# Down stage of a fused block kernel: W11 loaded once into the tile that becomes T1, T2 and T4, ten places in turn for the other blocks, T4's sums begun in P3

## The chip, the cores and the metric

One Trainium2 chip, one core. The metric is the device time of one execution in microseconds (us); lower is better.

## What is computed

The reference is one transformer block on x (512 x 2048, fp32): AdaLN modulation, a convolution mixer and a sparse attention mixer, an output projection, and a gated feed-forward network. The change touches only the last matrix product, the one with ffn_w2:

```python
h = modulate(rms_norm(x, norm_ffn[l]), sh_f, sc_f)
x = x + g_f[:, None, :] * ((silu(h @ ffn_w1[l]) * (h @ ffn_w3[l])) @ ffn_w2[l])   # ffn_w2: 5632 x 2048
```

## The kernel before

The stage for the last product, here the down stage, multiplies the gated activations (512 x 5632, spilled to DRAM as `gd` by the stage before it, here the up stage) by `ffn_w2`. It splits both into 2 x 2 blocks and forms seven products P1 to P7 in place of eight (Strassen's scheme in Winograd's form). The 5632 rows of `ffn_w2` are cut into four groups b = 0 to 3 (`GS = (5, 6, 6, 5)`). In each group a block of the weight has 5 or 6 tiles of 128 x 1024 (512 KB), indexed j. The order of the products is 1, 2, 5, 6, 3, 7, 4 in group 0 and 1, 5, 6, 3, 7, 2, 4 in the others. One tile of one product is a unit (b, p, j): 12 matmuls of 512 columns on PE. There are 154 units, written out in `units`; the loop at the end of the listing walks over them.

What a product needs of the weight: P1 takes W11, P2 takes W21, P3 takes W22, P5 takes T1, P6 takes T2 and P4 takes T4. T1 is W11 + W12 (the plain load of W11 on SP's queue, then an accumulating DMA of W12 on POOL's queue), T2 is T1 + W22 (a DVE addition, `w_sum`), T4 is T2 + W21 (an accumulating DMA on POOL's queue). All three are the same tile `t` in turn. P7 takes T3 = W12 + W22, a load on SP's queue and an accumulating DMA on POOL's queue into a tile of its own. (`"t3"` in the code; the sums' signs lie in the other operand.)

Every unit's weight tile is then split by `w_split`: ACT casts it to the matmul's type (`whi`, `w_hi`, L948), DVE subtracts (`wlo`, L1262). `hi` and `lo` have three buffers each, so the split of unit n + 2 can begin when PE has done with unit n - 1. The activations are split in the same way by `a_parts` (`ghi` on ACT, `glo` on DVE), and `evict` adds the PSUM banks to the output tiles on DVE after each product.

Where the tiles lie: W11 in `ring[0]` (tag raw, 4 places, shared with the up stage), t in `tz` (6 places), and W22, T3 and W21 in `wz` (tag w, 6 places). `tz`, `wz` and the activations' parts lie in memory that the up stage's operands hC1 to hC7 have held. `AHEAD` says how many units ahead of its own a tile's load is written in the program (W11 4, T1 9, W22 6, T3 7, W21 6, T4's sum 10); within that, a scheduler orders each engine's queue, and a load waits until the last reader of its place is done. SP's and POOL's queues issue in order: an issue that waits holds back what stands behind it. `r`, `gd` and `gf` on SP's queue are the up stage's spill, the residual and the gate; `k` on POOL's queue is the load of the next group's activations.

Of the kernel before, what the change touches and what calls it, by code (L numbers as in the profile page):

```python
# [9 lines left out]
F32 = mybir.dt.float32  # L10
# [3 lines left out]
ALU = mybir.AluOpType  # L14
# [3 lines left out]
P = 128  # L18
# [51 lines left out]
def block_kernel(ctx: ExitStack, tc: tile.TileContext, a: dict, out: bass.AP):  # L70
    nc = tc.nc
# [4 lines left out]
    def pool(name, bufs=1, stack=ctx, **kw):  # L76
        return stack.enter_context(tc.tile_pool(name=name, bufs=bufs, reuse_waits="tile", **kw))
# [4 lines left out]
    def rings(stack, raw, split):  # L82
        return (pool("raw", raw, stack=stack), pool("hi", split, stack=stack), pool("lo", split, stack=stack))
# [42 lines left out]
    ring = rings(ctx, 4, 3)  # L126
# [752 lines left out]
    for n in range(4):  # L879
# [8 lines left out]
        for i, ps in enumerate(pst):  # L888
            t = tp.tile([P, 512], F32, tag="t", name="t")
# [56 lines left out]
    def w_hi(t):  # L946
        hi = ring[1].tile([P, HK * P], F32R, tag="hi", name="whi")
        nc.scalar.copy(hi, t)  # L948
        return hi
# [156 lines left out]
    GS, GM, HN = (5, 6, 6, 5), 6, D // 2  # L1106
# [4 lines left out]
    def k_load(b, half):  # L1111
        n = GS[b]
        t = kraw[b, half] = krp.tile([P, GM, S], F32, tag=f"k{half}", name=f"k{half}")
        for j in range(n):
            nc.gpsimd.dma_start(t[:, j, :], gd[START[b] + half * n + j])
# [73 lines left out]
    tz = pool("tz", GM)  # L1189
    wz = pool("wz", 6)  # L1190
# [4 lines left out]
    W, A_, bank = {}, {}, {}  # L1195

    def a_parts(b, p):

        with tc.issue_after(W["last"]) if W.get("last") else ExitStack():
            a_parts_(b, p)  # L1200
# [26 lines left out]
    def w_load(b, p, j):  # L1227
        f = (START[b] + j, START[b] + GS[b] + j)

        def block(r, c):  # L1230
            return w2[f[r] * P:(f[r] + 1) * P, c * HN:(c + 1) * HN]

        def get(pl, tag, one, plus=None):
            t = pl.tile([P, HN], F32, tag=tag, name=tag)
            nc.sync.dma_start(t, one)
            if plus is not None:
                nc.gpsimd.dma_start(t, plus, accum_op=ALU.add)
            return t

        if p == 1:  # L1240
            W[b, 11, j] = get(ring[0], "raw", block(0, 0))
        elif p == 5:
            W[b, "t", j] = get(tz, "t", block(0, 0), block(0, 1))
        elif p == 6:
            W[b, 22, j] = get(wz, "w", block(1, 1))
        elif p == 7:
            W[b, "t3", j] = get(wz, "w", block(0, 1), block(1, 1))
        elif p == 2:
            W[b, 21, j] = get(wz, "w", block(1, 0))
        elif p == 4:  # L1250
            nc.gpsimd.dma_start(W[b, "t", j], block(1, 0), accum_op=ALU.add)

    def w_sum(b, p, j):
        if p == 6:
            t = W[b, "t", j]
            nc.vector.tensor_add(t, t, W[b, 22, j])

    def w_split(b, p, j):
        t = W[b, {1: 11, 5: "t", 6: "t", 3: 22, 7: "t3", 2: 21, 4: "t"}[p], j]
        hi = w_hi(t)  # L1260
        lo = ring[2].tile([P, HN], F32R, tag="lo", name="wlo")
        W["last"] = nc.vector.tensor_sub(lo, t, hi.bitcast(F32)).ins  # L1262
        W[b, p, j] = hi, lo
# [5 lines left out]
    def multiply(b, p, js, done=None):  # L1269
        name, make = banks(b, p)  # L1270
        if 0 in js and p in (1, 5, 2):
            bank[name] = [make() for _ in range(4)]
        ps = bank[name]
        ahi, alo = A_[b, p]
        for t in range(2):
            tok = slice(t * P, (t + 1) * P)
            for c in range(2):
                cs = slice(c * 512, (c + 1) * 512)
                for j in js:
                    hi, lo = W[b, p, j]  # L1280
                    for m, (x_, w) in enumerate(((ahi, lo), (alo, hi), (ahi, hi))):
                        nc.tensor.matmul(ps[2 * t + c], x_[:, j, tok], w[:, cs],  # L1282
                                         start=m == 0 and j == 0 and p in (1, 5, 2),
                                         stop=m == 2 and j == GS[b] - 1 and p in (3, 2, 4), skip_group_check=True)
                if done:
                    done(t, c)

    def evict(b, p):
        last = b == NG - 1
        r, c = {1: (0, 0), 2: (0, 0), 6: (0, 1), 3: (0, 1), 5: (1, 1), 7: (1, 1), 4: (1, 0)}[p]  # L1290
        if b == 0 and p == 1:
            return
        for t in range(2):
            for h in range(2):
                cs = slice(c * HN + h * 512, c * HN + (h + 1) * 512)
                y = y2[2 * r + t][:, cs]
                ps = bank[banks(b, p)[0]][2 * t + h]
                if b == 0 and p in (2, 5, 6, 4):
                    nc.scalar.copy(y, ps)
                else:  # L1300
                    nc.vector.tensor_add(y, ps, y)
                if last and p in (3, 7, 2):
                    nc.vector.scalar_tensor_tensor(y, y, -1.0 if c else 1.0, gf[:, cs], op0=ALU.mult, op1=ALU.mult)
            if last and p in (3, 7, 2):
                i = 2 * r + t
                nc.gpsimd.dma_start(out[0, i * P:(i + 1) * P, c * HN:(c + 1) * HN], y2[i][:, c * HN:(c + 1) * HN],
                                    accum_op=ALU.add)
        if b == 0 and p == 2:

            for t in range(2):  # L1310
                for h in range(2):
                    y = y2[t][:, h * 512:(h + 1) * 512]
                    nc.vector.tensor_add(y, bank["x"][2 * t + h], y)

    def last_block():

        for t in range(2):
            for h in range(2):
                cs = slice(h * 512, (h + 1) * 512)
                y = y2[2 + t][:, cs]  # L1320
                r = dp.tile([P, 512], F32, tag=f"d{1 + h}", name="r")
                nc.sync.dma_start(r, xd[h][:, t, :])
                nc.vector.tensor_mul(y, y, gf[:, cs])
                nc.vector.tensor_add(y, y, r)
# [8 lines left out]

    prods = [(b, p) for b in range(NG) for p in ((1, 5, 6, 3, 7, 2, 4) if b else (1, 2, 5, 6, 3, 7, 4))]
    units = [(b, p, j) for b, p in prods for j in range(GS[b])]
    AHEAD = {1: 4, 5: 9, 6: 6, 7: 7, 2: 6, 4: 10}

    def loads(n):
        for m in range(n + 13, n + 3, -1):
            if 0 <= m < len(units):  # L1340
                b, p, j = units[m]
                if (12 if (b, p) == (0, 5) else AHEAD.get(p)) == m - n:
                    w_load(b, p, j)

    for n in range(-13, 0):
        loads(n)
    for m in range(2):
        w_split(*units[m])
    a_parts(*prods[0])
    with tc.issue_after(A_["last"]), tc.issue_after(A_["first"]):  # L1350
        order[-1]["post"](order[-1])
# [2 lines left out]
    for n, (b, p, j) in enumerate(units):  # L1354
        last = b == NG - 1
        if j == 0:
            q += 1
            if q + 2 < len(prods):
                a_parts(*prods[q + 2])
        if j == 2:  # L1360
            if not last and p == 3:
                k_load(b + 1, 0)
            elif not last and q % 7 == 5:
                k_load(b + 1, 1)
            elif last and p == 6:
                gf = krp.tile([P, GM, S], F32, tag="k0", name="k0").rearrange("p j s -> p (j s)")[:, :D]
                nc.sync.dma_start(gf, gfd.to_broadcast([P, D]))
        loads(n)
        if n + 4 < len(units):
            w_sum(*units[n + 4])  # L1370
        if n + 2 < len(units):
            w_split(*units[n + 2])
        if last and p == 4:
            if j == 0:
                last_block()
            if j < GS[b] - 3:
                multiply(b, p, [j])
            elif j == GS[b] - 1:
                multiply(b, p, [j - 2, j - 1, j], last_tile)
            continue  # L1380
        multiply(b, p, [j])
        if j == GS[b] - 1:
            evict(b, p)
# [24 lines left out]
```

## Time and profile before

| | |
|---|---|
| median of 3 runs | 2261.0 us (2258.97 to 2263.16) |
| the profiled execution's own time | 2263.49 us |
| its span, first to last instruction | 2261.7 us |
| PE busy | 96% of the span |
| mean granted clock of TensorE | 0.991 of full speed |
| first and last matmul of the down stage | 1792.42 and 2256.8 us |

The span is what the trace covers; the execution's own time is 1.8 us longer. PE's busy time is modelled from the starts of its matmuls. An engine's idle time matters here only where PE waits for it in the end.

### The profile page before, as it was taken

How to read it: one execution, taken by the hardware profiler on the slowest of the kernel's cores; microseconds unless marked ns; L12 is line 12 of the kernel's file. 1: busy time of each engine (PE TensorE's matmuls, PEld its weight loads, DVE VectorE, ACT ScalarE, POOL GpSimd, SP SyncE). 2: the span in 40 equal slices, each digit the busy share in tenths (PEclk: the TensorE clock that was granted, in tenths of full speed). 3: DMA queues.
4: the chain of work that ended last, by engine and by line, in shares of the span. 5: the costliest groups of instructions: out<-in, count | busy, mean ns of one | idle time of the engine just before them, and what ended most of it. 6: DMA issues, size and time to landing. Idle time of an engine off the chain costs nothing.

```text
span 2261.7 us, 30554 instructions
## 1 busy us (share of the span) xinstructions
PE 2182.5 (96%) x11377; PEld 1812.0 (80%) x11377; DVE 1725.9 (76%) x2523; ACT 996.1 (44%) x1558; POOL 222.4 (10%) x267
## 2 busy tenths in 40 slices
PE   6999999999999999899999999999999998999998
PEld 5788778778777787788888888888888876777786
DVE  6878877877769755977878777887878776778697
ACT  5335235554444222744444444444444454444442
POOL 5310000000000000010000000000000121211111
PEclk9999999999999999999999999999999999999999
DMA  9965766544446865397776767677775699786966
GB/s 319 363 219 178 260 198 189 165 143 137 135 138 223 296 233 160 104 224 174 180 183 165 184 170 179 165 177 172 182 182 135 208 292 264 180 265 176 265 155 161
DMA packets 441096, 446.72 MB, mean 198 GB/s; under 512 B 18232, under 2 KB 345116, under 8 KB 440308
## 3 DMA queue, kind: packets, MB, share of 16 engines
q1 hardware_dynamic: 371764, 330.40, 46.7%
q0 software_dynamic: 69040, 114.12, 23.6%
q8 instruction: 89, 1.46, 0.3%
q14 instruction: 59, 0.48, 0.1%
q10 hardware_dynamic: 144, 0.26, 0.0%
HBM read 424.78 MB, written 19.93 MB: 197 GB/s over the span
## 4 chain that ended last, share of the span: by engine, by line
PE 73%; DMA 12%; DVE 11%; issue 2%; ACT 1%; POOL 0%; SPq 0%; DVEq 0%; ACTq 0%; POOLq 0%
PE main L960 14%; PE aux L960 10%; PE main L962 7%; PE main L98 6%; PE main L100 6%; PE main L99 6%; PE aux L1282 5%; PE aux L962 5%; DMA araw<-in_ada_w 5%; PE main L1282 5%; DMA w<-in_ffn_w 5%; DVE acc L185 2%; DVE wlo L1262 2%; PE aux L98 1%; DMA raw<-in_ffn_w 1%
## 5 line engine op out<-in xcount | busy, mean ns | idle before, releaser
L948 ACT CAST whi<-raw 128x1024 fp32r<-128x1024 f32 x282 | 295.3, 1047 | 351.5 <-PE main L960 114.0
L953 DVE TENSOR_TENSOR wlo<-raw,whi 128x1024 fp32r<-128x1024 f32 x260 | 315.4, 1218 | 81.2 <-ACT whi L948 80.8
L960 PE MATMUL main<-hC,whi 128*128 128x512 f32 x1408 | 356.7, 395 | 5.2 <-DVE hC L977 3.7
L960 PEld LDWEIGHTS main<-hC,whi 128*128 128x128 f32 x1408 | 255.1, 190 | 51.9 <-DVE hC L977 4.3
L960 PE MATMUL aux<-hC,whi 128*128 128x512 f32 x1072 | 270.1, 393 | 0.0
L185 DVE SCALAR_TENSOR_TENSOR acc<-araw,cT,acc 128x512 f32<-128x512 f32 x248 | 185.6, 748 | 73.2 <-DMA araw<-in_ada_w 60.2
L960 PEld LDWEIGHTS aux<-hC,whi 128*128 128x128 f32 x1072 | 193.7, 190 | 34.9
L962 PEld LDWEIGHTS main<-hC,wlo 128*128 128x128 f32 x1408 | 192.1, 190 | 13.8
L962 PE MATMUL main<-hC,wlo 128*128 128x256 f32 x1408 | 196.3, 282 | 0.0
L98 PE MATMUL main<-alo,whi 128*128 128x512 f32 x448 | 182.8, 408 | 1.4 <-DVE alo L347 1.4
L948 ACT CAST whi<-t 128x1024 fp32r<-128x1024 f32 x108 | 113.5, 1052 | 152.7 <-PE aux L1282 42.1
L99 PE MATMUL main<-ahi,wlo 128*128 128x512 f32 x448 | 176.6, 394 | 0.0
L100 PE MATMUL main<-ahi,whi 128*128 128x512 f32 x448 | 176.5, 395 | 0.0
L92 ACT CAST whi<-raw 128x1024 fp32r<-128x1024 f32 (+2 forms) x84 | 79.5, 949 | 207.0 <-PE main L100 138.6
L962 PEld LDWEIGHTS aux<-hC,wlo 128*128 128x128 f32 x1072 | 146.3, 190 | 12.4 <-DVE wlo L953 1.9
L98 PE MATMUL main<-wlo,ahi 128*128 128x512 f32 x384 | 152.9, 398 | 0.0
L99 PE MATMUL main<-whi,alo 128*128 128x512 f32 x384 | 151.8, 395 | 0.0
L962 PE MATMUL aux<-hC,wlo 128*128 128x256 f32 x1072 | 149.9, 282 | 1.5 <-DVE wlo L953 1.5
L100 PE MATMUL main<-whi,ahi 128*128 128x512 f32 x384 | 151.1, 394 | 0.0
L1262 DVE TENSOR_TENSOR wlo<-w,whi 128x1024 fp32r<-128x1024 f32 x66 | 79.9, 1222 | 81.3 <-ACT whi L948 81.2
L1282 PE MATMUL aux<-wlo,ghi 128*128 128x512 f32 x308 | 123.1, 400 | 16.2 <-DVE wlo L1262 16.2
L1049 DVE TENSOR_TENSOR raw<-raw 128x1024 f32<-128x1024 f32 x84 | 102.3, 1218 | 47.1 <-DMA raw<-in_ffn_w 47.0
(317 smaller groups left out, 4069.5 us busy)
## 6 DMA issues: line engine op xcount, KB each, us to landing
raw<-in_ffn_w SPq DMA_DIRECT2D x219, 512.0 KB, 4.9
araw<-in_ada_w SPq DMA_DIRECT2D x176, 256.0 KB, 3.0
w<-in_ffn_w SPq DMA_DIRECT2D x66, 512.0 KB, 8.0
t<-in_ffn_w POOLq DMA_DIRECT2D x65, 512.0 KB, 8.5
araw<-in_ada_w POOLq DMA_DIRECT2D x56, 512.0 KB, 14.4
raw<-in_w_in SPq DMA_DIRECT2D x128, 192.0 KB, 2.7
t<-in_ffn_w SPq DMA_DIRECT2D x43, 512.0 KB, 5.7
araw<-in_ada_w SPq DMA_DIRECT2D x40, 512.0 KB, 5.4
```

Source lines behind the costliest of these rows:

```text
L92: nc.scalar.copy(hi[:, :m], raw[:, :m])
L98: nc.tensor.matmul(ps, lhs[0], rhs[1], start=first, stop=False)
L99: nc.tensor.matmul(ps, lhs[1], rhs[0], start=False, stop=False)
L100: nc.tensor.matmul(ps, lhs[0], rhs[0], start=False, stop=last)
L185: nc.vector.scalar_tensor_tensor(acc, w, s, acc, op0=ALU.mult, op1=ALU.add)
L948: nc.scalar.copy(hi, t)
L953: nc.vector.tensor_sub(lo, t, hi.bitcast(F32))
L960: nc.tensor.matmul(ps, wt[0][:, ks[k]], hC[p][:, k, :], start=first and k == 0, stop=False, skip_group_check=True)
L962: nc.tensor.matmul(ps[:, HS:], wt[1][:, ks[k]], hC[p][:, k, 0:HS], start=False, stop=last and k == HK - 1, skip_group_check=True)
L1049: nc.vector.tensor_add(to, x, y)
L1262: W["last"] = nc.vector.tensor_sub(lo, t, hi.bitcast(F32)).ins
L1282: nc.tensor.matmul(ps[2 * t + c], x_[:, j, tok], w[:, cs], start=m == 0 and j == 0 and p in (1, 5, 2), stop=m == 2 and j == GS[b] - 1 and ...
```

## The change

W11 is loaded by `w_load` for P1 straight into the tile t, P1 splits it there, and right behind the split of each P1 unit POOL is given the accumulating DMA that makes T1 of it (`split`). The separate load of W11 for T1 is gone: 22 loads of 512 KB fewer. W22, T3 and W21 take ten places in turn, four in `ring[0]` and six in `wz` (`place`). The leads are longer: W11 5, W22 9, T3 12, W21 9 (7 in group 0), T4's sum 15 (14 in group 0), so that it is written beside P3.

```diff
--- before.py
+++ after.py
@@ -1230,23 +1230,26 @@
         def block(r, c):
             return w2[f[r] * P:(f[r] + 1) * P, c * HN:(c + 1) * HN]
 
-        def get(pl, tag, one, plus=None):
-            t = pl.tile([P, HN], F32, tag=tag, name=tag)
+        def place():
+            W["n"] = W.get("n", -1) + 1
+            pl, tag = (ring[0], "raw") if W["n"] % 10 < 4 else (wz, "w")
+            return pl.tile([P, HN], F32, tag=tag, name=tag)
+
+        def get(t, one):
             nc.sync.dma_start(t, one)
-            if plus is not None:
-                nc.gpsimd.dma_start(t, plus, accum_op=ALU.add)
             return t
 
         if p == 1:
-            W[b, 11, j] = get(ring[0], "raw", block(0, 0))
+            W[b, "t", j] = get(tz.tile([P, HN], F32, tag="t", name="t"), block(0, 0))
         elif p == 5:
-            W[b, "t", j] = get(tz, "t", block(0, 0), block(0, 1))
+            nc.gpsimd.dma_start(W[b, "t", j], block(0, 1), accum_op=ALU.add)
         elif p == 6:
-            W[b, 22, j] = get(wz, "w", block(1, 1))
+            W[b, 22, j] = get(place(), block(1, 1))
         elif p == 7:
-            W[b, "t3", j] = get(wz, "w", block(0, 1), block(1, 1))
+            t = W[b, "t3", j] = get(place(), block(0, 1))
+            nc.gpsimd.dma_start(t, block(1, 1), accum_op=ALU.add)
         elif p == 2:
-            W[b, 21, j] = get(wz, "w", block(1, 0))
+            W[b, 21, j] = get(place(), block(1, 0))
         elif p == 4:
             nc.gpsimd.dma_start(W[b, "t", j], block(1, 0), accum_op=ALU.add)
 
@@ -1256,7 +1259,7 @@
             nc.vector.tensor_add(t, t, W[b, 22, j])
 
     def w_split(b, p, j):
-        t = W[b, {1: 11, 5: "t", 6: "t", 3: 22, 7: "t3", 2: 21, 4: "t"}[p], j]
+        t = W[b, {1: "t", 5: "t", 6: "t", 3: 22, 7: "t3", 2: 21, 4: "t"}[p], j]
         hi = w_hi(t)
         lo = ring[2].tile([P, HN], F32R, tag="lo", name="wlo")
         W["last"] = nc.vector.tensor_sub(lo, t, hi.bitcast(F32)).ins
@@ -1333,19 +1336,24 @@
 
     prods = [(b, p) for b in range(NG) for p in ((1, 5, 6, 3, 7, 2, 4) if b else (1, 2, 5, 6, 3, 7, 4))]
     units = [(b, p, j) for b, p in prods for j in range(GS[b])]
-    AHEAD = {1: 4, 5: 9, 6: 6, 7: 7, 2: 6, 4: 10}
+    AHEAD = {1: 5, 6: 9, 7: 12, 2: 9, 4: 15}
 
     def loads(n):
-        for m in range(n + 13, n + 3, -1):
+        for m in range(n + 16, n + 3, -1):
             if 0 <= m < len(units):
                 b, p, j = units[m]
-                if (12 if (b, p) == (0, 5) else AHEAD.get(p)) == m - n:
+                if (7 if (b, p) == (0, 2) else 14 if b == 0 and p == 4 else AHEAD.get(p)) == m - n:
                     w_load(b, p, j)
 
-    for n in range(-13, 0):
+    def split(n):
+        w_split(*units[n])
+        if units[n][1] == 1:
+            w_load(units[n][0], 5, units[n][2])
+
+    for n in range(-16, 0):
         loads(n)
     for m in range(2):
-        w_split(*units[m])
+        split(m)
     a_parts(*prods[0])
     with tc.issue_after(A_["last"]), tc.issue_after(A_["first"]):
         order[-1]["post"](order[-1])
@@ -1369,7 +1377,7 @@
         if n + 4 < len(units):
             w_sum(*units[n + 4])
         if n + 2 < len(units):
-            w_split(*units[n + 2])
+            split(n + 2)
         if last and p == 4:
             if j == 0:
                 last_block()
```

SP's queue where the up stage ends, before: raw_16056 and raw_16058 (ahead of these rows), raw_16063, raw_16070 and raw_16104 are W11 of group 0; raw_16728 is W11 of group 1, t_16060 and t_16065 the first tiles of T1, w_16068 the first of W21.

```order
L1235 DMA raw_16063<-in_ffn_w2 128x1024
L1012 DMA gd42_6762<-d2_15719 128x512
L1322 DMA r_19113<-xd0_6718 128x512
L1322 DMA r_19117<-xd1_6719 128x512
L1235 DMA raw_16070<-in_ffn_w2 128x1024
L1235 DMA raw_16104<-in_ffn_w2 128x1024
L1235 DMA raw_16728<-in_ffn_w2 128x1024
L1235 DMA t_16060<-in_ffn_w2 128x1024
L1235 DMA t_16065<-in_ffn_w2 128x1024
L1235 DMA w_16068<-in_ffn_w2 128x1024
```

The same place now: raw_16099 and raw_16122 are the third and fourth tile of W21, the five t are W11 of group 0, w_16141 is the last tile of W21, w_16217 the first of W22.

```order
L1239 DMA raw_16099<-in_ffn_w2 128x1024
L1012 DMA gd42_6762<-d2_15719 128x512
L1325 DMA r_19069<-xd0_6718 128x512
L1325 DMA r_19073<-xd1_6719 128x512
L1239 DMA raw_16122<-in_ffn_w2 128x1024
L1239 DMA t_16056<-in_ffn_w2 128x1024
L1239 DMA t_16058<-in_ffn_w2 128x1024
L1239 DMA t_16060<-in_ffn_w2 128x1024
L1239 DMA t_16064<-in_ffn_w2 128x1024
L1239 DMA t_16068<-in_ffn_w2 128x1024
L1239 DMA w_16141<-in_ffn_w2 128x1024
L1239 DMA w_16217<-in_ffn_w2 128x1024
```

W21 has moved ahead of W11, and the first tile of W11, which stood first, now stands behind the fourth of the `raw` loads.

DVE's queue at the same time, before: wlo_16074, wlo_16078 and wlo_16108 are P1's units 0 to 2, glo_16081 is P1's activations, glo_16090 P2's and glo_16096 P5's; d1 and d2 belong to the up stage's last tile.

```order
L1262 TENSOR_TENSOR wlo_16078<-raw_16058,whi_16076 128x1024
L967 TENSOR_TENSOR d1_15861<-aux_15997,d1_15861 128x256
L1213 TENSOR_TENSOR e_16093<-k1_15928,k0_15922 128x1280
L1262 TENSOR_TENSOR wlo_16108<-raw_16063,whi_16106 128x1024
L1224 TENSOR_TENSOR glo_16081<-k0_15922,ghi_16080 128x1280
L971 TENSOR_TENSOR d1_15861<-main_15844,d1_15861 128x256
L1224 TENSOR_TENSOR glo_16090<-k1_15928,ghi_16089 128x1280
L1079 SCALAR_TENSOR_TENSOR d2_15885<-d2_15885,d1_15861 128x512
L1224 TENSOR_TENSOR glo_16096<-e_16093,ghi_16095 128x1280
```

And now, where wlo_16072, wlo_16077 and wlo_16103 are P1's units 0 to 2:

```order
L967 TENSOR_TENSOR d1_15861<-aux_15997,d1_15861 128x256 x2
L1265 TENSOR_TENSOR wlo_16072<-t_16056,whi_16070 128x1024
L1265 TENSOR_TENSOR wlo_16077<-t_16058,whi_16075 128x1024
L1224 TENSOR_TENSOR glo_16081<-k0_15922,ghi_16080 128x1280
L971 TENSOR_TENSOR d1_15861<-main_15844,d1_15861 128x256
L1224 TENSOR_TENSOR glo_16090<-k1_15928,ghi_16089 128x1280
L1079 SCALAR_TENSOR_TENSOR d2_15885<-d2_15885,d1_15861 128x512
L1213 TENSOR_TENSOR e_16093<-k1_15928,k0_15922 128x1280
L1265 TENSOR_TENSOR wlo_16103<-t_16060,whi_16101 128x1024
```

P1's activations now follow two splits of W11 tiles that the changed SP queue has loaded late. Behind these rows DVE's order is the same in both kernels to the end.

SP's queue ahead of group 1, before: t_16843 and t_16864 are the last tiles of T1 of group 1, raw_16821 and raw_16846 of its W11; the four raw_17... are W11 of group 2, and w_17147, w_17174 the first tiles of T3 of group 1.

```order
L1235 DMA t_16843<-in_ffn_w2 128x1024
L1235 DMA t_16864<-in_ffn_w2 128x1024
L1235 DMA raw_16821<-in_ffn_w2 128x1024
L1235 DMA raw_16846<-in_ffn_w2 128x1024
L1235 DMA raw_17571<-in_ffn_w2 128x1024
L1235 DMA raw_17592<-in_ffn_w2 128x1024
L1235 DMA raw_17613<-in_ffn_w2 128x1024
L1235 DMA raw_17634<-in_ffn_w2 128x1024
L1235 DMA w_17147<-in_ffn_w2 128x1024
L1235 DMA w_17174<-in_ffn_w2 128x1024
```

And now: raw_17043 to w_17102 are the first four tiles of T3 of group 1, the five t its W11 tiles 1 to 5, w_17121 and w_17140 the last two of T3.

```order
L1239 DMA raw_17043<-in_ffn_w2 128x1024
L1239 DMA raw_17063<-in_ffn_w2 128x1024
L1239 DMA raw_17083<-in_ffn_w2 128x1024
L1239 DMA w_17102<-in_ffn_w2 128x1024
L1239 DMA t_16720<-in_ffn_w2 128x1024
L1239 DMA t_16738<-in_ffn_w2 128x1024
L1239 DMA t_16756<-in_ffn_w2 128x1024
L1239 DMA t_16775<-in_ffn_w2 128x1024
L1239 DMA t_16803<-in_ffn_w2 128x1024
L1239 DMA w_17121<-in_ffn_w2 128x1024
L1239 DMA w_17140<-in_ffn_w2 128x1024
```

Four of the six T3 loads have moved from behind the next group's first W11 loads to ahead of their own group's W11.

## Rows read from the trace of the kernel before

**Rows 1.** The page: PE's line of part 1 (busy us, share of the span, instructions) and part 4, the chain that ended last, by engine.

```profile
PE 2182.5 (96%) x11377; PEld 1812.0 (80%) x11377; DVE 1725.9 (76%) x2523; ACT 996.1 (44%) x1558; POOL 222.4 (10%) x267
...
PE 73%; DMA 12%; DVE 11%; issue 2%; ACT 1%; POOL 0%; SPq 0%; DVEq 0%; ACTq 0%; POOLq 0%
```

**Rows 2.** Who waited for whom from 1790 to 2262 us: us in total, times, longest.

```profile
ACT whi L948 <- DMA w<-in_ffn_w: 80.8, 25, 7.4
...
PE aux L1282 <- DVE wlo L1262: 16.2, 12, 3.7
PE main L1282 <- DVE wlo L1262: 14.7, 12, 4.7
```

**Rows 3.** PE's matmuls of the down stage (L1282) in stretches that begin and end at the first matmul of a unit: the stretch, its length, PE busy (matmuls), granted clock, DMA share, GB/s. In order: P1 and P2 of group 0; P5, P6 and P3 of group 0; P7 of group 0 with two units of P4; P6 of group 1; the last unit of P3 with P7 of group 1; P1, P5 and P6 of group 2; the last unit of P3 with P7 of group 2; P6 and P7 of group 3.

```profile
1792.42:1807.02 14.60, 14.03 (x61) 1.00 1.01 285
1807.02:1826.94 19.92, 15.81 (x62) 0.91 1.04 322
1826.94:1867.74 40.80, 40.80 (x182) 1.00 1.00 276
1867.74:1897.35 29.61, 22.15 (x85) 0.88 0.83 250
...
1938.15:1955.88 17.73, 16.82 (x73) 1.00 0.88 198
...
1969.48:1995.66 26.18, 20.86 (x86) 1.00 1.05 310
...
2028.30:2046.08 17.78, 16.90 (x73) 1.00 1.03 299
2046.08:2062.97 16.89, 16.61 (x73) 1.00 0.01 4
2062.97:2081.27 18.30, 16.91 (x73) 1.00 0.88 184
...
2094.87:2120.80 25.93, 20.85 (x86) 1.00 1.03 302
...
2180.64:2195.24 14.60, 13.94 (x62) 1.00 0.83 176
...
2208.84:2229.58 20.74, 15.78 (x62) 0.92 0.95 238
```

**Rows 4.** The chain of waits from 1852 to 1884 us (start us, us, what), and the time from issue to landing of the loads of L1235 (SP) and of the accumulating DMAs of L1237 (POOL).

```profile
1853.96 9.69 DMA w<-in_ffn_w
...
1867.53 14.13 DMA w<-in_ffn_w
...
DMA to landing us min/median/max: 3.8/6.5/22.0
...
DMA to landing us min/median/max: 5.4/9.2/15.1
```

**Rows 5.** The DMA view from 1790 to 2262 us: queue, packets, MB, share of the 16 engines' time. q0 is POOL's queue, q1 SP's.

```profile
q0 software_dynamic: 13088, 46.67, 47.9%
q1 hardware_dynamic: 16133, 57.70, 33.3%
```

**Rows 6.** Where the up stage ends and the down stage begins: SP's issues, PE, DVE and ACT in order of time (start us, us, line, what, count, idle before).

```profile
1785.10 4.83 SPq L1235 DMA_DIRECT2D raw<-in_ffn_w  x3
...
1789.66 1.11 PE L962 MATMUL main<-hC,wlo 128*128 128x256 f32 x8
1792.42 0.96 PE L1282 MATMUL main<-wlo,ghi 128*128 128x512 f32 x3 [1.65 <-ACT ghi L1223]
1793.95 0.50 PE L1282 MATMUL main<-whi,glo 128*128 128x512 f32 x1 [0.57 <-DVE glo L1224]
...
1792.40 1.49 DVE L1224 TENSOR_TENSOR glo<-k,ghi 128x1280 fp32r<-128x1280 f32 x1
...
1797.55 1.22 DVE L1262 TENSOR_TENSOR wlo<-raw,whi 128x1024 fp32r<-128x1024 f32 x1
...
1789.86 1.05 ACT L948 CAST whi<-raw 128x1024 fp32r<-128x1024 f32 x1 [1.70 <-PE main L960]
...
1791.13 1.24 ACT L1223 CAST ghi<-k 128x1280 fp32r<-128x1280 f32 x1
1792.28 0.36 ACT L970 COPY d<-main 128x256 f32<-128x256 f32 x1
```

**Rows 7.** PE's first matmul behind an idle stretch (idle us and releaser in brackets), and the granted clock behind it (stretch, length, PE busy, clock, DMA share, GB/s).

```profile
1816.32 0.50 PE L1282 MATMUL aux<-wlo,ghi 128*128 128x512 f32 x1 [3.71 <-DVE wlo L1262]
...
1792.42:1796.13 3.71, 3.14 (x12) 1.00 0.96 304
1816.32:1820.80 4.48, 4.48 (x12) 0.62 1.04 338
```

**Rows 8.** DVE around P7 of group 3, in order of time.

```profile
2207.25 0.68 DVE L1301 TENSOR_TENSOR y<-main,y 128x512 f32<-128x512 f32 x1
...
2212.82 0.69 DVE L1303 SCALAR_TENSOR_TENSOR y<-y,k 128x512 f32<-128x512 f32 x1
...
2218.42 2.35 DVE L1262 TENSOR_TENSOR wlo<-w,whi 128x1024 fp32r<-128x1024 f32 x2
```

**Rows 9.** The split of P4's first tile in group 2 (DVE) and the cast of P1's first tile in group 3 (ACT), six units later.

```profile
2132.96 1.22 DVE L1262 TENSOR_TENSOR wlo<-t,whi 128x1024 fp32r<-128x1024 f32 x1 [1.50 <-ACT whi L948]
...
2148.20 1.05 ACT L948 CAST whi<-raw 128x1024 fp32r<-128x1024 f32 x1 [1.67 <-PE main L1282]
```

## The prediction

> **What bounds the kernel now.** I read the chain that ended last first: PE holds 73% of it and is busy for 96% of the span [rows 1], so a change gains what PE waits, and no more. The change is confined to the down stage, so I read next who waited for whom there: PE waits for the DVE half of the weight's split, 16.2 + 14.7 us in 24 waits, and behind that split stands ACT's cast, which waits 80.8 us for loads into the `w` places [rows 2]. The third view says where. Cut at unit borders, a stretch without a stall makes 15 units in 40.80 us, 2.72 us each; what a stretch takes above 2.72 per unit is loss, waits and a lower clock together [rows 3]:
>
> - P1 of group 0, 5 units: 14.60 - 13.60 = 1.0. P2 of group 0, 5 units: 19.92 - 13.60 = 6.3.
> - P7 with its neighbours, by group: 7 units 29.61 - 19.04 = 10.6; 7 units 26.18 - 19.04 = 7.1; 7 units 25.93 - 19.04 = 6.9; 5 units 20.74 - 13.60 = 7.1. Together 31.7.
> - P1 and P5 of group 2, 6 units each: 1.5 and 0.6.
> - P6 of groups 1 to 3 (6, 6, 5 units): 1.4, 2.0 and 1.0. Together 4.4.
>
> That is 45.5 us in all, and 31.7 of them belong to T3. The chain says why [rows 4]: a T3 tile waits until P3's split has freed its `w` place, then takes 9.69 us for its load and, later, 14.13 us for its accumulation. P3's unit j is split six units ahead of P7's unit j, so some 16 us are there for what takes 24.
>
> **The change part by part.** T3 (31.7 us). With ten places the first four T3 tiles of groups 1 and 2, and all five of groups 0 and 3, go into places whose readers are P7 and P2 of the group before, or P2 of the same group; the order of SP's queue shows four of them loaded ahead of W11. Only tiles 4 and 5 of groups 1 and 2 still wait for P3's first two splits. They are needed 10 units later, some 27 us, against a load and an accumulation of 9.69 + 14.13 at the worst seen above, 6.5 + 9.2 at the median [rows 4]. I take the whole T3 loss as gone but for one place: in group 3, DVE's order stands. From the end of P7's second split six half-tile operations, a `glo` and one more half tile run before the third split: 2218.42 - 2212.82 = 5.6 us, and they cannot start before P3's matmuls are nearly done [rows 8]. P3 ends at 2208.84. With T3 in time the second split follows the eviction of the first bank, 2207.25 + 0.68, and ends at 2209.1; the third then begins at 2214.7 and ends at 2215.9, where PE wants it at 2208.84 + 5.44 = 2214.3. So 1.6 us of the 31.7 stay: -30.1.
>
> P2 of group 0 (6.3 us). W21 is now the first thing loaded, while the up stage still runs, three tiles of it into places that W11 had. The loss goes: -6.3.
>
> P1 and P5 of group 2 (2.1 us). These are W11 tiles that came late into the four `raw` places, and what followed. Now W11 has six places and five units' lead. -2.1.
>
> P6 (4.4 us). There DVE has eviction, `w_sum` and the split in a row; its order is the same, so I leave it: 0. If late T data had a share in it, up to 4.4 more would go.
>
> The start. This is the price. SP issues the fourth `raw` load at 1785.10, behind the up stage's last split of its own [rows 6], and that wait stays. W11's first tile now stands behind it, at about 1785.5, where it used to be the first. With the fastest landing, 3.8 us [rows 4], for the load ahead and 1.43 us for each one behind it (below), it lands at 1790.4, the second at 1791.8. ACT first does P1's `ghi`, which has been ready, then at 1790.8, when the last up product ends (1789.66 + 1.11), the copy (0.36) and the second `ghi` (1.24), to 1792.4; then the casts, 1.05 each, to 1793.5 and 1794.5 [rows 6]. DVE: splits to 1794.7 and 1795.95, and only then P1's `glo`, 1.49, to 1797.45. PE's second matmul group needs that `glo`; it came at 1793.95 before [rows 6]. So +3.5. The loads are no tighter than the casts as long as they land within 7 us; at the median they do, at 22.0 they would cost 15 more.
>
> The clock at the start. PE idles 3.9 us until the first split and 1.8 us more for `glo`. Behind an idle 3.71 us the granted clock was 0.62 of full speed, so mostly the lower of its two levels, 1.2 GHz, for 4.48 us, which costs 0.38 x 4.48 = 1.7; behind 1.65 us it stayed at 1.00 [rows 7]. The bounds are 0 and 2.2 (4.48 us wholly at half speed); 3.9 is nearest to 3.71: I take +1.7. [...]
>
> What is queued where. POOL's accumulation for T1 waits for P1's split, and behind it on POOL stand T3's of group 0, T4's and the next group's `k`; each of them is due over 20 us later than it is freed. The 22 loads dropped free DMA time: of 472 us, q1's 33.3% is 157 us for 57.70 MB, so 1.43 us of all 16 engines per 512 KB load, and q0's 47.9% is 226 us for 46.67 MB, so 2.54 us per accumulation [rows 5]. 22 x 1.43 = 31 us go of 383. That gives PE nothing by itself: from 2046.08 to 2062.97 the DMA share was 0.01 while PE went on [rows 3]. The engines' total falls to 352 us in a stage that shrinks to some 430, so 82% as before. T1's accumulations come one per unit, 2.54 in 2.72 us, and need five units; they fit with SP idle there.
>
> The sum: -30.1 - 6.3 - 2.1 + 3.5 + 1.7 = -33.3 us. The profiled execution's own time is 2263.49, so 2230.2; the median of the runs is 2.5 lower, 2261.0, so **2228**. A measurement of this kernel tells 0.2% from no change, some 4.5 us.
>
> **The rivals.** Slower, by one mechanism at three places: W11's tile j of the next group can be loaded only when P4's split of tile j is done, since it is the same place. In group 2 that split ends at 2134.2 and the cast that needs the next tile came at 2148.2 [rows 9], 14.0 us; PE feels it 2.9 us later, the unit starting 5.24 behind its cast's start, of which cast and split take 2.3. So a W11 load may take 16.9 us. The median is 6.5, but 22.0 occurs [rows 4], when SP's loads and POOL's accumulations share the engines, 1.43 + 2.54 = 3.97 us per pair. The four T3 loads and their accumulations now run just ahead of W11: four pairs are 16 us, on the edge. If W11 had eight pairs ahead of it, 32 us, each of the three group changes would lose 15 us and 1.7 for the clock, 50 us: 2278. It decides from 26 us: three times 9.4 us late and 1.7 for the clock take the 33 us back. Against it: the T3 loads are freed one per unit and ahead of W11's, each pair costs 3.97 us for 2.72 of a unit, so four units leave a backlog of 5 us, not 16. The Trainium skill (DMA: Bandwidth & Descriptors, Issuing engines are not separate DMA queues) has it that DMAs of all issuing engines run on the same 16 engines and interleave, which is what speaks for this rival; the 22.0 and a share of 1.04 beside P2 of group 0 agree. I give it 0.05.
>
> Half the gain of T3: tiles 4 and 5 of groups 1 and 2, queued on POOL behind six accumulations for T4 and six `k` loads (15 + 8 us of DMA time, taking `k` as half a tile each), still come late, and the full DMA share of group 0 delays its T3 or its successor's W11. Half of 7.1 + 6.9 stays and 3 us in group 0: 2238. The 27 us window against 16 to 24 speaks against it. 0.17.
>
> The start goes wrong: W11's five loads meet the backlog that made 22.0 us, and the first tile lands 15 us late: 2243. Against it: POOL has no accumulation to issue until the first split. 0.04. No change in the end, as all of T3's gain is lost to such waits: 2261, 0.04. That the change does not do what it says can be ruled out where it counts: the order of SP's queue has T3 ahead.
>
> **How the numbers follow.** My forecast has 0.70 and spans 2220 (no clock loss, no rest in group 3, P6 gone: -7.7) to 2235; with the second and third rival up to 2246 less than 0.1 is left out above and little below: 2219 to 2246. Faster: 0.70 + 0.17 + 0.04 = 0.91; same 0.04; slower 0.05.
>
> **What would show it.** In the changed profile P7's stretches should take 2.72 us per unit but for a stall of 1.6 us at group 3's third unit; P2 of group 0 should have none; the second matmul group of P1 should begin at about 1797.5 behind a `glo`, with a granted clock below 1 behind it; P6's 4.4 us should be there still; SP's `ffn_w` loads should be 22 fewer. The forecast is wrong if ACT's cast of P1's or T3's tiles waits for DMA by more than some us at the group changes, or if the start of P1 waits for the load of t rather than for `glo`.

## The result and the profile after

The changed kernel takes 2232.8 us (median of 4 runs, 2229.6 to 2239.2), the kernel before 2261.1 (4 runs, 2259.0 to 2263.2): ratio 0.9879, 95% interval 0.9855 to 0.9902, so it is 1.2% faster. On another chip, with the same file, it was 2235.6 against 2266.6, 0.9859 (0.9844 to 0.9874). The profiled execution's own time is 2229.62 us, 3.2 below its median, its span 2227.9; against the profiled execution of before, 2263.49, that is 33.9 less.

The page of the changed kernel, PE's line of part 1 and the chain by engine, answers to [rows 1]:

```profile
PE 2172.0 (97%) x11377; PEld 1809.7 (81%) x11377; DVE 1726.3 (77%) x2523; ACT 997.4 (45%) x1558; POOL 222.5 (10%) x267
...
PE 75%; DVE 12%; DMA 9%; issue 2%; ACT 1%; SPq 0%; POOL 0%; DVEq 0%; ACTq 0%; POOLq 0%
```

PE's work is the same; most of what the span lost is time in which PE was idle. Its busy time fell by 10.5 us all the same, as matmuls behind a stall count for longer, partly at a lower clock: P7 of group 0 with two units of P4 had 22.15 us of busy time for 7 units, 19.04 us of work, at a clock of 0.88 [rows 3]. Who waited for whom from 1790 us on (us in total, times, longest) answers to [rows 2]:

```profile
PE main L1285 <- DVE wlo L1265: 4.9, 2, 4.0
PE aux L1285 <- DVE wlo L1265: 3.0, 3, 1.4
...
ACT whi L948 <- DMA t<-in_ffn_w: 0.9, 2, 0.7
```

ACT's casts waited 80.8 us for loads into the `w` places; no such row is left, and 0.9 us for two loads of t is all that casts of the weight now wait for loads. SP issues 88 loads of `ffn_w2`, where it issued 110. PE's wait for `wlo` fell from 30.9 us to 7.9. Where what is left lies, the matmuls by product show (stretch, length, PE busy and matmuls, granted clock, DMA share, GB/s; P1 and P2 of group 0, P7 of group 0, P6 and P7 of group 1, P7 of group 2, P6 and P7 of group 3), against [rows 3]:

```profile
1793.61:1812.15 18.54, 17.48 (x60) 0.77 1.05 308
1812.15:1825.75 13.60, 13.60 (x61) 1.00 1.04 339
1866.55:1880.15 13.60, 13.60 (x61) 1.00 0.91 273
1926.51:1944.23 17.72, 16.80 (x74) 1.00 0.87 192
1960.55:1976.87 16.32, 16.32 (x74) 1.00 0.99 354
...
2076.19:2092.51 16.32, 16.32 (x74) 1.00 0.94 335
2152.35:2166.91 14.56, 13.90 (x62) 1.00 0.79 171
2180.51:2195.83 15.32, 13.89 (x62) 1.00 0.42 68
```

Five units at 2.72 us are 13.60, six are 16.32. P2 of group 0 and P7 of groups 0, 1 and 2 stand exactly there; P7 of group 3 has 1.7 us too many, P6 of groups 1 to 3 has 1.4, 1.4 and 1.0, and P1 of group 0 has 4.9 where it had 1.0. The rest has 0.1 (P4 of group 0). So the losses went from 45.5 us to 10.5; the idle time ahead of the first matmul, below, is not among them.

The start, engine by engine (start us, us, what, idle before and its releaser), answers to [rows 6]:

```profile
1788.49 1.11 PE L962 MATMUL main<-hC,wlo 128*128 128x256 f32 x8
1793.61 1.65 PE L1285 MATMUL main<-wlo,ghi 128*128 128x512 f32 x3 [4.01 <-DVE wlo L1265]
1796.32 0.76 PE L1285 MATMUL main<-whi,glo 128*128 128x512 f32 x1 [1.06 <-DVE glo L1224]
...
1792.33 2.44 DVE L1265 TENSOR_TENSOR wlo<-t,whi 128x1024 fp32r<-128x1024 f32 x2 [4.59 <-ACT whi L948]
1794.69 1.48 DVE L1224 TENSOR_TENSOR glo<-k,ghi 128x1280 fp32r<-128x1280 f32 x1
...
1789.64 0.37 ACT L970 COPY d<-main 128x256 f32<-128x256 f32 x1 [0.30 <-PE main L962]
1790.10 1.26 ACT L1223 CAST ghi<-k 128x1280 fp32r<-128x1280 f32 x1
1791.26 1.04 ACT L948 CAST whi<-t 128x1024 fp32r<-128x1024 f32 x1
1792.47 1.04 ACT L948 CAST whi<-t 128x1024 fp32r<-128x1024 f32 x1 [0.17 <-DMA t<-in_ffn_w]
```

And the granted clock there (the same columns as above), against [rows 7]:

```profile
1793.61:1796.32 2.71, 1.65 (x3) 0.50 1.01 373
1796.32:1802.02 5.70, 5.70 (x14) 0.50 1.04 318
1802.02:1806.02 4.00, 4.00 (x18) 0.97 1.06 285
```

PE is idle 4.01 us where it was 1.65, then waits for `glo` behind two splits, and its first 17 matmuls run at the lower of the two levels, 1.2 GHz.

DVE around P7 of group 3, in order of time, answers to [rows 8]:

```profile
2179.52 1.22 DVE L1265 TENSOR_TENSOR wlo<-w,whi 128x1024 fp32r<-128x1024 f32 x1
...
2186.26 2.36 DVE L1265 TENSOR_TENSOR wlo<-w,whi 128x1024 fp32r<-128x1024 f32 x2
```

The second split now follows the first bank's eviction at once, and the third begins 5.5 us behind its end, 5.6 before. It ends at 2187.5, and PE wanted it two units behind P7's start, at 2180.51 + 5.44 = 2185.95: that is the 1.7 us that P7 has left there, but for some 0.2.

### The profile page after: what moved, and what is told of

Read it like the earlier page. It is cut to its first block, busy times and chain, and to the rows that moved or that the text cites. A ratio compares the mean times of both kernels' runs of the same rounds, so it can differ in the third digit from the quotient of the medians.

```text
span 2227.9 us, 30520 instructions
## 1 busy us (share of the span) xinstructions
PE 2172.0 (97%) x11377; PEld 1809.7 (81%) x11377; DVE 1726.3 (77%) x2523; ACT 997.4 (45%) x1558; POOL 222.5 (10%) x267
## 4 chain that ended last, share of the span: by engine, by line
PE 75%; DVE 12%; DMA 9%; issue 2%; ACT 1%; SPq 0%; POOL 0%; DVEq 0%; ACTq 0%; POOLq 0%
PE main L960 14%; PE aux L960 10%; DMA araw<-in_ada_w 7%; PE aux L1285 7%; PE main L1285 7%; PE main L962 7%; PE aux L962 5%; PE main L98 5%; PE main L100 5%; PE main L99 5%; DVE acc L185 2%; DVE wlo L1265 2%; PE aux L768 1%; PE aux L98 1%; PE aux L100 1%
## 5 line engine op out<-in xcount | busy, mean ns | idle before, releaser
L948 ACT CAST whi<-raw 128x1024 fp32r<-128x1024 f32 x288 | 301.7, 1048 | 354.5 <-PE main L960 110.4
L948 ACT CAST whi<-t 128x1024 fp32r<-128x1024 f32 x130 | 136.8, 1052 | 186.1 <-PE main L1285 57.0
L1265 DVE TENSOR_TENSOR wlo<-t,whi 128x1024 fp32r<-128x1024 f32 x88 | 106.3, 1222 | 30.0 <-ACT whi L948 29.9
L1285 PE MATMUL main<-wlo,ghi 128*128 128x512 f32 x308 | 121.4, 395 | 4.9 <-DVE wlo L1265 4.9
```

Of the source, the lines that this page charges most:

```text
L1285: nc.tensor.matmul(ps[2 * t + c], x_[:, j, tok], w[:, cs], start=m == 0 and j == 0 and p in (1, 5, 2), stop=m == 2 and j == GS[b] - 1 and ...
```

## The experiments

Times are medians in us. Three groups of runs (e1 to e4, e5 to e8, e9 and e10) each have their own runs of the kernel before on the same chip, so ratios are compared across groups and times within one.

| run | time | before | ratio (95%) |
|---|---|---|---|
| e1: six places, old leads, W11 once | 2264.2 | 2266.1 | 0.9989 (0.9977 to 1.0001) |
| e2: six places, new leads, W11 once | 2264.4 | 2266.1 | 0.9994 (0.9985 to 1.0003) |
| e3: ten places, old leads, W11 once | 2236.7 | 2266.1 | 0.9876 (0.9861 to 0.9891) |
| e4: the change with 22 loads put back | 2247.6 | 2266.1 | 0.9925 (0.9909 to 0.9942) |
| e5: the change again | 2235.6 | 2266.6 | 0.9859 (0.9844 to 0.9874) |
| e6: W11 of group 0 first | 2231.6 | 2266.6 | 0.9838 (0.9821 to 0.9855) |
| e7: DVE work put later | 2231.3 | 2266.6 | 0.9846 (0.9830 to 0.9861) |
| e8: e6 and e7 | 2224.4 | 2266.6 | 0.9812 (0.9791 to 0.9832) |
| e9: seven places | 2251.7 | 2267.8 | 0.9927 (0.9905 to 0.9949) |
| e10: eight places | 2236.9 | 2267.8 | 0.9866 (0.9849 to 0.9882) |

### Places, leads or fewer loads (e1 to e3)

The theory was that T3 came late for want of places; the rivals, that the longer leads or the smaller DMA traffic brought it in time. The three edits against the changed kernel:

```diff
# e1 and e2: six places
-            W["n"] = W.get("n", -1) + 1
-            pl, tag = (ring[0], "raw") if W["n"] % 10 < 4 else (wz, "w")
-            return pl.tile([P, HN], F32, tag=tag, name=tag)
+            return wz.tile([P, HN], F32, tag="w", name="w")
# e1 and e3: leads as before
-    AHEAD = {1: 5, 6: 9, 7: 12, 2: 9, 4: 15}
+    AHEAD = {1: 5, 6: 6, 7: 7, 2: 6, 4: 10}
...
-                if (7 if (b, p) == (0, 2) else 14 if b == 0 and p == 4 else AHEAD.get(p)) == m - n:
+                if AHEAD.get(p) == m - n:
```

> Undoes the places and the leads, keeps W11 loaded once: W22, T3 and W21 in six places, leads 6, 7, 6 and 10 as before, ring[0] not used. If the gain is the places (my theory), the T3 loss of some 7 us per group stays (28 to 31.7 in all), while P2 of group 0 (6.3) is cured, since no W11 load of group 1 stands ahead of W21 on SP; W11's first tile no longer stands behind the fourth raw load, so the start costs between 1.7 and 5.2: 2254 to 2262. If the gain is the 22 dropped loads (less DMA traffic), T3 comes in time with six places too: 2226 to 2236.

> As the last, but with the long leads of the change (9, 12, 9, T4's sum 15). If the places decide, T3 still waits for P3's split and a longer lead in the program gives nothing: 2252 to 2262, T3's loads still landing some 20 us after P3's splits. If the leads decide (T4's sums begun in P3, out of T3's way), P7's stretches go to 2.72 us per unit and the time to 2228 to 2238.

> The ten places with the leads of before (W22 6, T3 7, W21 6, T4's sum 10). If the places decide: 2230 to 2238, no stall in P7 but the 1.6 us of group 3. If the leads decide: 2250 or more, P7 stalling some 7 us in each group.

With six places the time is that of before, by either leads; with ten it is the change's, by either leads. P7 of groups 0 to 3 in e1:

```profile
1873.02:1896.59 23.57, 17.43 (x61) 0.86 0.91 274
1977.71:1999.96 22.25, 17.96 (x73) 1.00 1.04 313
2100.57:2121.57 21.00, 17.63 (x72) 1.00 1.05 309
2209.56:2230.28 20.72, 15.80 (x61) 0.92 0.94 241
```

That is 10.0, 5.9, 4.7 and 7.1 us above 2.72 per unit, and 2.0 more in the last units of P3: 29.7 us of T3 loss, although W11 is loaded once. In e2 it is 27.8 in all. In e3 P7 of groups 0 to 2 has nothing and group 3 the known 1.7; here groups 1 and 3:

```profile
1970.16:1986.48 16.32, 16.32 (x74) 1.00 0.97 348
...
2190.12:2205.44 15.32, 13.89 (x62) 1.00 0.44 68
```

So the places decide, and the leads, T4's sums begun in P3 among them, cannot be seen in the time. "W11 loaded once" by itself (e1) gains P2 of group 0 and the stalls of P1 and P5 in group 2, 8.4 us, and pays 5.0 of that back at the start (2.3 in the first gap, 2.6 in P1); its time is within 0.3% of before. The first gap of e1:

```profile
1801.40 1.65 PE L1283 MATMUL main<-wlo,ghi 128*128 128x512 f32 x3 [3.99 <-DVE wlo L1263]
```

### What the 22 loads cost when T3 is in time (e4)

```diff
         def get(t, one):
-            nc.sync.dma_start(t, one)
+            W["w11" if p == 1 else "-", b, j] = nc.sync.dma_start(t, one).ins
...
         elif p == 5:
+            with tc.issue_after(W["w11", b, j]):
+                nc.sync.dma_start(dram.tile([P, HN], F32, name=f"dz{b}{j}"), block(0, 0))
             nc.gpsimd.dma_start(W[b, "t", j], block(0, 1), accum_op=ALU.add)
```

> The changed kernel with 22 loads of W11 put back on SP's queue, each behind W11's own load, into DRAM tiles that nothing reads. If DMA traffic gives PE nothing: as the changed kernel, 2231 to 2239 (at the start the first of these loads stands between W11's tiles, up to 3 us). If the 22 dropped loads are what T3 gained from: most of 28 us comes back, 2250 or more.

It was neither: 10.8 us slower than e3, which ran beside it and equals the change. SP's queue, q1, carries as much as before again, against [rows 5]:

```profile
q1 hardware_dynamic: 16152, 57.74, 32.8%
```

Counted as above, its stage loses 21.6 us where e3's loses 10.5. The difference lies in group 0's P7 (21.96 - 13.60 = 8.4 us) and in P1 and P5 of group 1 (2.9); P7 of groups 1 and 2 stands at 16.32. T3 is not what is late. The stretch, then DVE and POOL there, and the chain:

```profile
1867.68:1889.64 21.96, 15.90 (x62) 0.84 0.86 283
```

```profile
1876.39 1.76 DVE L1224 TENSOR_TENSOR glo<-k,ghi 128x1536 fp32r<-128x1536 f32 x1 [6.93 <-DMA k<-gd]
1878.06 2.35 DVE L1267 TENSOR_TENSOR wlo<-raw,whi 128x1024 fp32r<-128x1024 f32 x2
...
1859.96 0.54 POOL L1115 DMA_DIRECT2D k<-gd  x1 [3.28 <-DMA t<-in_ffn_w]
```

```profile
1838.98 14.11 DMA t<-in_ffn_w
...
1853.38 18.52 DMA k<-gd
```

DVE holds P7's third split behind the `glo` of the next group's P1, and that `glo` waits for `k`; PE is idle for 6.06 us, and the clock behind the stall adds the rest. POOL's DMAs take eight semaphores in turn, so an issue waits until the DMA eight before it has landed: the `k` issue at 1853.38 follows the accumulation for T4 that began at 1838.98 and took 14.1 us to land, and that `k` load then takes 18.5. From 1840 to 1880 us the accumulations for T4 take 16.3 us to land in the median and the `k` loads 14.7; in the same stretch of the change it is 7.1 and 9.8. The Trainium skill (DMA: Bandwidth & Descriptors, Issuing engines are not separate DMA queues) says that DMAs of all issuers interleave on the same 16 engines. The landing times of e4 agree: loads on SP's queue made POOL's slower. The mean DMA share of these 40 us does not tell the two apart (0.98 and 0.97).

The added loads end in DRAM and stand at other places in SP's queue than the 22 old ones, so 10.8 us is the price of as much traffic, and only about that of the old loads. With ten places the smaller traffic is worth that much, and without it the change keeps 18.6 us of e3's 29.4; with six (e1) T3 stays late without those loads too.

### How many places (e9, e10)

```diff
-    wz = pool("wz", 6)
+    wz = pool("wz", 4)   # e9: 3
...
-            pl, tag = (ring[0], "raw") if W["n"] % 10 < 4 else (wz, "w")
+            pl, tag = (ring[0], "raw") if W["n"] % 8 < 4 else (wz, "w")   # e9: % 7
```

> The changed kernel with seven shared places (four raw, three w). A T3 tile that waits for P3 then has 7 units, 19.0 us, from that split to its own need, where six places gave 16.3 and ten give 27.2. With six, P3 and P7 lost 29.7 us in all four groups, some 7.4 each, so T3 needs about 16.3 + 7.4 = 24 us. If the time from freed place to need is what counts, each place more gives back 2.72 us per group until nothing is left: 29.7 - 10.9 = 19 us stay here, 1.7 in the change, so 17 us slower than the change, 0.9945 of the kernel before. If it is the common rotation (T3 of one product in places of another) that counts and not their number, the time is the change's, 0.986 to 0.988.

> The same with eight places (four raw, four w): 8 units, 21.8 us. By the count 29.7 - 21.8 = 8 us stay, 6 more than in the change, 0.9895. By the rotation alone 0.986 to 0.988, with 1.7 us in P7 of group 3 only.

P7 of groups 0 to 3 with seven places, and of groups 1 to 3 with eight (13.60 us in group 0):

```profile
1867.71:1890.61 22.90, 16.32 (x61) 0.85 0.82 270
1970.95:1992.18 21.23, 18.86 (x73) 0.92 1.05 327
2091.51:2112.66 21.15, 17.49 (x73) 1.00 1.02 304
2200.65:2215.97 15.32, 13.90 (x62) 1.00 0.98 251
```

```profile
1961.17:1977.56 16.39, 16.39 (x73) 1.00 1.04 335
2076.89:2094.19 17.30, 16.66 (x73) 1.00 1.04 332
2182.19:2197.55 15.36, 13.94 (x62) 1.00 0.75 185
```

Seven leave 9.3 + 4.9 + 4.8 + 1.7 = 20.7 us where 19 were expected, eight 0.0 + 0.1 + 1.0 + 1.8 = 2.9 where 8 were, and the time with eight is the change's, 0.9866 where the count gave 0.9895. So it is the number that counts, as e9 shows, but not at 2.72 us per place: 29.7, 20.7, 2.9 and 1.7 us with six, seven, eight and ten. Eight units from a freed place, 21.8 us, are nearly enough for T3, where I had worked out 24 from the loss with six. The 9.3 us of seven in group 0 are one tile, and the clock of 0.85 behind it: its accumulation stands on POOL behind five `k` issues and takes 17.0 us, as its chain shows.

```profile
1865.83 17.04 DMA raw<-in_ffn_w
```

### The start, and DVE behind an eviction (e5 to e8)

e6 puts group 0's t into the places that are free before the up stage ends:

```diff
+            if b == 0:
+                pl, tag = (wz, "w") if p in (1, 6) else (tz, "t")
+                if p == 1 and j < 4:
+                    pl, tag = ring[0], "raw"
+            else:
...
-            W[b, "t", j] = get(tz.tile([P, HN], F32, tag="t", name="t"), block(0, 0))
+            W[b, "t", j] = get(tz.tile([P, HN], F32, tag="t", name="t") if b else place(), block(0, 0))
```

e7 moves the activations of P7, and the gating of P3's output in group 3 (`gate3` holds the two `scalar_tensor_tensor` and the output DMA of one token tile, taken out of `evict`):

```diff
-            if q + 2 < len(prods):
+            if q + 2 < len(prods) and p != 6:
                 a_parts(*prods[q + 2])
+        if j == 3 and p == 6:
+            a_parts(*prods[q + 2])
...
+        if last and p == 7 and j in (2, 3):
+            gate3(j - 2)
```

> The changed kernel itself, timed beside the next three on one chip: 0.986 to 0.990 of the kernel before; per unit the same losses as in its first profile (P1 of group 0 5, P6 3.7, P7 of group 3 1.7).

> Only the start: in group 0 four of the t tiles lie in the raw places and the fifth in a w place, so that W11 is loaded and split ahead of the up stage's end as before; W21 and T3 of group 0 take the t places in turn, W22 the other w places. If the start costs what I worked out (3.5 for glo behind two late splits and 1.7 for the clock), it goes back by 5: 0.9855 against 0.988 for the change, some 2228; PE's second matmul group again 1.5 us behind the first, at a granted clock of 1.00. If the start is set by something that the order does not touch (loads of t, the up stage's end), the time stays at the change's. If the raw places, held by t to the end of group 0, are what group 1's T3 needs, 3 to 7 us come back there.

> Only DVE's order: the subtraction and the glo for P7 are written at the fourth unit of P6 rather than at its first, and the multiplication of P3's output by the gate in group 3 is written at P7's third and fourth unit. If P6's 3.7 us and P7's 1.6 us in group 3 are DVE's backlog behind an eviction, both go: 5 us less than the change, some 2228, ratio 0.9855. If late T data have the larger share of P6, its 3.7 us stay and only 1.7 go.

> Both edits together. If they are independent: 10 us less than the change, some 2223, ratio 0.983; no stretch of the stage above 2.72 us per unit but the first unit.

e7's P6 of group 1 (those of groups 2 and 3 are as clean) and its P7 of group 3:

```profile
1930.31:1946.63 16.32, 16.32 (x73) 1.00 1.01 184
...
2180.55:2195.07 14.52, 13.90 (x62) 1.00 0.32 53
```

P6's loss is gone to the last 0.1 us, so none of it was late data; of P7's 1.7 us 0.9 stay, behind the four additions of the eviction and `glo`. By the ratios e6 is 4.8 us faster than the change (0.0021 of 2266.6), e7 2.9, both 10.7, where 5, 5 and 10 were expected. Singly the intervals overlap the change's, so neither gain by itself is clear of the noise; together they do not, and e8 beats both kernels. In e8's profile 0.8 us of P7 of group 3 stay too. e6 starts with the gap of before, 1.65 us, but not at the clock of 1.00 that was expected. Its start (PE, then the clock), and that of e8:

```profile
1793.04 0.97 PE L1290 MATMUL main<-wlo,ghi 128*128 128x512 f32 x3 [1.65 <-ACT ghi L1223]
1794.56 0.80 PE L1290 MATMUL main<-whi,glo 128*128 128x512 f32 x1 [0.56 <-DVE glo L1224]
...
1793.04:1796.74 3.70, 3.14 (x8) 0.65 1.05 272
```

```profile
1795.41 0.97 PE L1290 MATMUL main<-wlo,ghi 128*128 128x512 f32 x3 [1.65 <-ACT ghi L1223]
1796.93 0.50 PE L1290 MATMUL main<-whi,glo 128*128 128x512 f32 x1 [0.56 <-DVE glo L1224]
...
1795.41:1799.11 3.70, 3.14 (x12) 1.00 1.07 277
```

The same idle times end once in the lower level and once not; that alone is 1.4 us between these two executions.

## Why the prediction was right

Its terms against the two profiled executions, by the stretches:

- **T3**, forecast -30.1: 31.7 to 1.7 us and 0.1 in group 0's P4, -29.9. The cause, that T3 waited for places that P3's splits free, is shown by e1 to e3, e9 and e10, and e4 shows that T3 is in time in ten places with the old amount of traffic too. The rest in group 3 was forecast at 1.6 from DVE's order and is 1.7, and e7 moves it by moving that order.
- **P2 of group 0**, -6.3: it has 13.60 us, so all of it went. **P1 and P5 of group 2**, -2.1: both went. e1 has both gains with six places and the old leads, and e4 has them with as much traffic as before, so they come with W11's leaving the `raw` places (its lead, 5 for 4, is in every run and not told apart). For P2 the prediction named W21's loading into those places; in e1 W21 lies in `w` places and P2 stands at 13.60 all the same.
- **P6**, 0: 4.4 became 3.8, and e7 shows that all of the 3.8 is DVE's order.
- **The start**: the second matmul group was put 3.5 us later against the up stage's end. It is: 1796.32 - 1789.60 = 6.7 us, against 1793.95 - 1790.77 = 3.2. The way there is the predicted one too: ACT's order sets it, two `ghi` and a copy ahead of the first cast, which then waits for no load, and `glo` behind two splits. The fourth `raw` load that stands ahead of W11 costs nothing, as forecast: in e1 none stands there and the first gap is 3.99 us all the same. PE idles 4.01 and 1.06 us where 3.9 and 1.8 were worked out; its first three matmuls, at the lower clock, took 0.7 us longer, which shortened the second wait.
- **The clock** was the term that was mis-sized: +1.7 with bounds of 0 and 2.2. Behind 4.01 us of idle time the clock is 0.50, not 0.62, until 1802.02. From the second matmul group to its end P1 takes 18.54 - 2.71 = 15.83 us where it took 14.60 - 1.53 = 13.07 before: 2.8 us, beyond the bound, as half speed over the 4.48 us of [rows 7] is no bound on how long the lower level lasts. The trace of before has a row at 0.50 throughout as well, behind 4.70 us, that the prediction did not weigh; it stands below. Other executions with a first gap of 4.0 us give for the same count 1.3 (e4) to 2.7 (e10), so what this term comes to is not fixed by the gap.
- **DMA traffic**, 0: that the 22 fewer loads give PE nothing was a wrong reading, and it cost the forecast nothing only because the change does drop them. e4 shows that with as much traffic as before 10.8 us of the gain would have been lost through `k`, which the prediction had due over 20 us later than it is freed. The share of 0.01 beside a PE that went on, from which it argued, shows that PE can do without DMA for 17 us, and not that a full share costs nothing elsewhere.

```profile
1884.12 0.80 PE L1282 MATMUL main<-wlo,ghi 128*128 128x512 f32 x1 [4.70 <-DVE wlo L1262]
...
1884.12:1888.50 4.38, 4.38 (x10) 0.50 0.36 137
```

The sum was -33.3; the profiled executions differ by 33.9. The terms above come to -29.9 - 6.3 - 2.0 - 0.6 + 3.5 + 2.8 = -32.5; 1.2 more is the up stage, which ended that much earlier in this execution (1789.60 against 1790.77) with nothing in the change to make it so. So the mechanism was right, but that the sum is right to 0.6 us is in part luck: 1.1 us too little for the clock and 1.2 us from the up stage nearly cancel.

The median moved less, 28.3 us, as the profiled execution of before lay 2.4 us above its median and that of the change 3.2 below. The forecast of 2228 took it that both lie 2.5 above, so it is 4.8 us too low. On the other chip the medians differ by 31.0 us. What sets an execution's place in that spread stays open; the clock at the start, 1.3 to 2.8 us by the executions above, can be one part of it.

Of the rivals, W11 late at the group changes did not show: no unit of P1 behind group 0 is above 2.72 us. Nor did half the T3 gain: tiles 4 and 5 of groups 1 and 2 were in time: in the trace of the change their accumulations land 5.8 to 7.3 us ahead of the casts that need them, over two units, which agrees with eight places being nearly enough. The loads at the start were not 15 us late.

## What to carry to other kernels

Count the units between the moment a place comes free and the moment its next tile is needed, and set it against load plus accumulation; a longer lead in the program gives nothing where the place is what is waited for. Look at the work that stands behind the late tile too: once T3 was in time, the next wait in line was the next group's activations, and it was the smaller traffic that kept it away. At the border of two stages compare the order of each engine's queue, not of the one that was changed alone: moving W11 to other places changed here the order on ACT and DVE as well, at a cost of 6.3 us by the profiles.

## What the runs showed of the hardware

- Behind 4.0 to 4.8 us of idle time (4.01 in the change, 4.70 before, 4.76 in e5) TensorE's granted clock was 0.50 of full speed, 1.2 GHz, for several us. The Trainium skill (TensorE: Matmul & The Clock Gate, What's actually happening) has throttled as the default that activity releases; these rows agree. Behind 1.65 and 0.56 us it was 1.00 in e8 and 0.65 in e6, with the same matmuls before it (44 in the 7.35 us ahead of the gap, at 1.00), so idle times of this length went either way.
- Accumulations that land in 5.4 us at the least [rows 4] took 14.1 in e4 and 17.0 in e9, where SP's loads and `k` ran beside them and the mean DMA share of these stretches was 1.07 and 1.00.
